# Thresholded attention with approximate screening: another table of the instruction order, and more spare products in the tail

## The chip, the cores and the metric

The kernel runs on one core of a Trainium2 chip. The metric is the device time of one launch in microseconds (us). A core has five engines with instruction streams of their own: TensorE (PE in the profile; PEld is its weight load), VectorE (DVE), ScalarE (ACT), GpSimd (POOL) and SyncE (SP, which here only issues DMAs). Each stream is executed in order; engines wait for each other and for DMAs through semaphores.

## The reference

For 8 x 12 heads, 512 queries and keys, and dimension 64:

```python
scores = np.einsum('bhqd,bhkd->bhqk', Q, K) / sqrt(64)
weights = softmax(scores)                      # over the keys
weights = np.where(weights > 0.1, weights, 0)
weights = weights / (weights.sum(-1) + 1e-10)
out = np.einsum('bhqk,bhkd->bhqd', weights, V)
```

With random normal inputs hardly any weight exceeds 0.1, so almost every row of the output is zero.

## The kernel before, in words

The kernel screens all rows cheaply, and computes exactly only those rows that may hold a weight over the threshold.

**The screen.** Work is cut into 24 *units* of four heads (two head pairs); unit 0 is loaded in two halves. For each unit, SP loads K (`k`, four DMAs at L398) and Q (`q`, L403) and writes zeros to that unit's part of the output (`z`, L626). POOL casts and scales Q to 16 bits (`qcast`, L411, two instructions). PE transposes K (`ktr`, L421) and Q (`qtr`, L432). ACT or DVE copies K from PSUM to a tile `kt` (`kev`), POOL casts it into the tile `qk` (`kh`, L391), and ACT or DVE copies Q there (`qev`; these copies stand at L387 for ACT and L389 for DVE). For each head pair and each quarter t of the keys, PE multiplies keys by queries (`sc`, L467, two matmuls), and ACT (L475) or DVE (L477) takes the exponential of each half (`ex`); which of the two does it is a letter of the table. PE then sums these exponentials and their eighth powers over the keys into one PSUM bank `acc` (`g`, L496). DVE also makes a bound of the row norms (`bits`, L457), which PE adds (`size`, L503).

**The exact part.** Four units (eight head pairs) form a *group*; there are six, called x0 to x5 here. When the 16 `g` and four `size` of a group are done, DVE reads `acc` (`evac`), and PE and DVE turn it into a list of at most 128 candidate rows (`test`, `flags`, `rank`, `key`, `oh`, `idx`, `idxev`). POOL gathers these rows of Q by an indirect DMA (`gather`, L556), spreads them (`split`, L563), PE transposes them (`xtr`, L568) and multiplies them by the group's keys in f32 (`xqk`, L582, 16 matmuls), ACT takes the exponential (`xexp`), and DVE finds the key over the threshold (`xcut`, `xkeep`, `xvi`, `xoi`). POOL then fetches the rows of V (`gv`, L612, indirect DMA, here called the *fetch*) and writes them over the zeros of the output (`scatter`, L619, indirect DMA), which has to wait until the fetch has landed. Both wait in POOL's stream, so that everything behind them on POOL, the casts `kh` and `qcast` of later units, waits with them.

**The order.** A string `ORDER` lists all 1138 steps: a number of the step, a letter of its engine (A, D, G, P, S for ACT, DVE, POOL, PE, SP), and buffer numbers. `Plan.run` walks through it:

```python
        for token in table.split():
            no, eng, at = re.fullmatch(r"(\d+)([A-Za-z])(.*)", token).groups()
            name, engs, deps, fn, takes, gives = self.ops[int(no)]
            ...
            fn(self.ENGINES[eng])
```

Every instruction is wrapped in `keep`, which asks the framework to hold it behind the one recorded before it on its engine. In the built program PE, DVE, ACT and SP stand exactly as the table lists them; on POOL some indirect DMAs stand one or more steps further ahead than in the table, both before and after the change.

**The tail.** After the last unit only the exact part of x4 and x5 is left, a chain of short steps. Into it the kernel puts products of zeros that nobody reads, which only keep PE busy, 3 behind `rank` of x5 and 14 behind its `idx`:

```python
    def spare(dst, n):
        for _ in range(n):
            keep(nc.tensor.matmul(dst[:], lhsT=idle[:, 0:P], rhs=idle[:], start=True, stop=True))
    ...
    add(("spare", 0), "PE", [("rank", last)], lambda e: spare(acc, 3))
    add(("spare", 1), "PE", [("idx", last)], lambda e: spare(acc, 14))
```

Of the kernel before, what the change touches and what calls it, by code (L numbers as in the profile page):

```python
# [23 lines left out]
182P 180D 181A 218P4.6.9 246D1 221P3.5.8 177A 252P0.2 186S 222A 223D 183P 253A4 220D 224P1.3.7 254A 227P0.5.6
251G0 187D1 332S1 226A 232P2.6.5 225A 229D 188P3 234A 247P 255G2 189D 256P1.5 219D 228A 190P 331S0 191D
235P0.6.4 257A 258D 293P3.4 192D1 236A 238P1.5.3 294D3 230P 295A 231P 239A 233D 296G1 240A 241P0.4.2 394S0
259P1.3.1 237D 242A 193P2 243D 292G1 261A 262P5.6.0 194D2 244P 260A 263D 248S 245P 264A 196G1 195D 287D0
# [54 lines left out]
class Plan:  # L82
# [28 lines left out]
def kernel(  # L111
# [232 lines left out]
    acc = psum.tile([P, SO * P], f32, name="acc")  # L344
# [32 lines left out]
    add = plan.add  # L377
# [455 lines left out]
```

## Time and profile before

| | |
|---|---|
| three runs | 199.59, 201.0, 201.52 us; median 201.0 us |
| the profiled execution | 201.37 us, of which the span from first to last instruction is 199.6 us |
| busy share of the span | PE 85%, DVE 80%, ACT 75%, POOL 43% |
| granted TensorE clock, mean | 0.951 |
| bytes moved by DMA | 38.45 MB; the loads and zero writes end at about 144 us |

The span has three parts: about 20 us until the pipeline is full, the screen up to about 176 us with the exact parts of x0 to x3 inside it, and a tail of 24 us in which the engines wait for each other. A row of a timeline gives start, duration, engine, line, operation, tiles and count, and in brackets the idle time of the engine ahead of it and what ended that. A row of a table of windows gives, for one stretch, the busy time of each engine (with the number of instructions), the granted clock (PEclk), the busy share of the DMA engines and GB/s.

### The profile page before, as it was taken

To read this page: it belongs to the slowest core of one execution; us is meant where nothing else is said; L and a number is where in the kernel's file an instruction comes from. 1 tells how busy PE (TensorE), PEld (TensorE's weight loads), DVE (VectorE), ACT (ScalarE), POOL (GpSimd) and SP (SyncE) were. 2 spreads that over 40 slices of the span, in tenths; PEclk is the share of its full clock that TensorE was granted. 3 is DMA by queue.
4 is the path that set the end of the run, shared out by engine and by line. 5 is a ranking of instruction groups with operands and counts; after the bars stand their busy time and mean duration, and the time that the engine had idled before them with its cause. 6 is when DMAs were issued, how large, how long until landed. Compare 5 with 4: busy or idle time off the path is not lost.

```text
span 199.6 us, 5872 instructions
## 1 busy us (share of the span) xinstructions
PE 169.8 (85%) x2266; PEld 69.7 (35%) x2266; DVE 160.3 (80%) x335; ACT 149.6 (75%) x303; POOL 86.6 (43%) x129
## 2 busy tenths in 40 slices
PE   7798999999899999999699999979729899977610
PEld 2343344443433434335234354334103534323100
DVE  7578999999799989999897999968907999972040
ACT  2769999999599999899597999958817898920010
POOL 8644435385085554342941855423440602305222
PEclk9979999999999999999999999999966999999785
DMA  5999999999899998999988768988800000000000
GB/s 139 254 252 255 302 283 255 338 324 287 247 247 347 325 291 181 272 275 236 252 231 256 221 183 242 288 290 227 361 4 0 5 0 3 7 0 11 1 2 10
DMA packets 67440, 38.45 MB, mean 193 GB/s; under 512 B 51882, under 2 KB 64240, under 8 KB 67408
## 3 DMA queue, kind: packets, MB, share of 16 engines
q1 hardware_dynamic: 66560, 37.50, 67.0%
q8 instruction: 19, 0.31, 0.7%
q0 software_dynamic: 576, 0.27, 0.6%
q10 hardware_dynamic: 272, 0.26, 0.5%
q14 instruction: 13, 0.11, 0.2%
HBM read 25.56 MB, written 12.78 MB: 192 GB/s over the span
## 4 chain that ended last, share of the span: by engine, by line
PE 44%; DVE 16%; ACT 13%; issue 11%; DMA 9%; POOL 4%; POOLq 0%; SPq 0%; DVEq 0%; ACTq 0%
PE bank L467 16%; PE acc L496 15%; ACT e L475 9%; DVE e L477 8%; PE bank L421 5%; PE bank L582 4%; DMA qs<-in_Q_dram,idx 4%; DMA vr<-in_V_dram,idx 4%; DVE v L457 3%; ACT kt L387 3%; DMA k<-in_K_dram 2%; POOL qk L391 2%; PE acc L503 2%; POOL out_dram L619 1%; DVE qk L389 1%
## 5 line engine op out<-in xcount | busy, mean ns | idle before, releaser
L475 ACT ACTIVATE e<-bank 128x512 f16<-128x512 f32 x232 | 121.5, 621 | 15.5 <-PE bank L467 15.1
L477 DVE TENSOR_SCALAR e<-bank 128x512 int16<-128x512 f32 x152 | 96.9, 680 | 10.1 <-PE bank L467 9.8
L467 PE MATMUL bank<-qk 64*128 64x512 f16 x384 | 68.0, 389 | 10.6 <-POOL qk L391 5.9
L496 PE MATMUL acc<-e,w_sum 128*32 128x512 f16 x384 | 57.8, 391 | 0.0
L496 PE MATMUL acc<-e,w_pow 128*32 128x512 bf16 x384 | 57.8, 391 | 0.0
L411 POOL TENSOR_SCALAR qh<-q 128x512 f16<-128x512 f32 x48 | 32.8, 683 | 17.1 <-DMA q<-in_Q_dram 13.0
L391 POOL CAST qk<-kt 128x1024 f16<-128x1024 f32 (+1 forms) x24 | 24.9, 1040 | 27.8 <-ACT kt L387 16.3
L467 PEld LDWEIGHTS <-qk 64*128 64x128 f16 x384 | 18.6, 95 | 47.8 <-issue 36.3
L387 ACT COPY kt<-bank 128x512 f32<-128x512 f32 (+1 forms) x35 | 19.9, 590 | 6.7 <-PE bank L421 6.5
L496 PEld LDWEIGHTS <-w_sum 128*32 128x32 f16 x384 | 13.8, 96 | 26.6 <-issue 22.1
L457 DVE TENSOR_SCALAR v<-qk 128x1024 int32<-128x1024 int32 x24 | 20.6, 860 | 2.8 <-POOL qk L391 1.1
L612 POOL DMA_INDIRECT vr<-in_V_dram,idx x6 | 7.2, 1193 | 27.9 <-DVE oks L738 6.4
L421 PE MATMUL bank<-identity_f,k 64*128 64x64 f32 x384 | 17.9, 233 | 0.4 <-DMA k<-in_K_dram 0.4
L421 PEld LDWEIGHTS bank<-identity_f,k 64*128 64x128 f32 x384 | 15.6, 145 | 6.2 <-issue 2.7
L496 PEld LDWEIGHTS <-w_pow 128*32 128x32 bf16 x384 | 13.6, 96 | 1.0 <-issue 0.7
L619 POOL DMA_INDIRECT out_dram<-vr,idx x6 | 6.7, 1120 | 15.7 <-PE bank L432 6.1
L582 PE MATMUL bank<-kt,xq 128*32 128x512 f32 x96 | 13.0, 663 | 0.4 <-ACT xq L387 0.4
L389 DVE COPY qk<-bank 128x512 f16<-128x512 f16 (+1 forms) x33 | 12.8, 409 | 0.4 <-PE bank L432 0.4
L556 POOL DMA_INDIRECT qs<-in_Q_dram,idx x6 | 7.1, 1188 | 10.6 <-DVE idx L546 8.1
L503 PE MATMUL acc<-v,w_size 128*32 128x512 bf16 x96 | 9.5, 385 | 1.8 <-DVE v L457 1.8
L432 PEld LDWEIGHTS <-qh 64*128 64x128 f16 x384 | 8.5, 95 | 6.1 <-issue 3.1
L432 PE MATMUL bank<-identity_h,qh 64*128 64x64 f16 x384 | 10.1, 191 | 0.5 <-POOL qh L411 0.2
(95 smaller groups left out, 105.1 us busy)
## 6 DMA issues: line engine op xcount, KB each, us to landing
k<-in_K_dram SPq DMA_DIRECT2D x96, 128.0 KB, 4.2
out_dram<-zero SPq DMA_DIRECT2D x24, 512.0 KB, 6.0
q<-in_Q_dram SPq DMA_DIRECT2D x23, 512.0 KB, 6.2
q<-in_Q_dram ACTq DMA_DIRECT2D x1, 256.0 KB
q<-in_Q_dram SPq DMA_DIRECT2D x1, 256.0 KB
qs<-in_Q_dram,idx POOLq DMA_INDIRECT x6, 4.8
vr<-in_V_dram,idx POOLq DMA_INDIRECT x6, 4.1
out_dram<-vr,idx POOLq DMA_INDIRECT x6, 3.6
```

What stands on the lines that cost most here:

```text
L387: keep(nc.scalar.copy(dst, src))
L389: keep(nc.vector.tensor_copy(dst, src))
L391: keep(nc.gpsimd.tensor_copy(dst, src))
L411: keep(nc.gpsimd.tensor_scalar(dst, src, ALPHA, 1.0, op0=ALU.mult, op1=ALU.mult))
L421: keep(nc.tensor.matmul(bank_at(("kp", u), i)[:, c:c + D], lhsT=src[ps, n0 + n, r, :], rhs=identity_f32[ps, ps], is_transpose=True, start= ...
L432: keep(nc.tensor.matmul(bank_at(("qp", u), i)[:].bitcast(f16)[:, c:c + D], lhsT=src[ps, n0 + n, r, :], rhs=identity_h[ps, ps], is_transpos ...
L457: keep(nc.vector.tensor_scalar(v_b[at("v", q)][:].rearrange("p a n c -> p (a n c)").bitcast(i32), qk_b[at("qk", q)][:].rearrange("p a n c ...
L467: keep(nc.tensor.matmul(bank_at(("sc", hp, t), h)[:], lhsT=qk[ps, 1, n, t * P:(t + 1) * P], rhs=qk[ps, 0, n, :], start=True, stop=True))
L475: keep(nc.scalar.activation(dst, src, ACTF.Exp, scale=math.log(2.0) / 1024.0, bias=exp_bias))
L477: keep(nc.vector.tensor_scalar(dst.bitcast(i16), src, EXP_BIAS * 1024.0, 0.0, op0=ALU.add, op1=ALU.max))
L496: keep(nc.tensor.matmul(acc[32 * j:32 * j + 32, :], lhsT=w, rhs=rhs, **turn(x, j)))
L582: keep(nc.tensor.matmul(bank_at(("xs", x))[32 * b:32 * b + 32, :], lhsT=xq[:, a * P + 32 * b:a * P + 32 * b + 32], rhs=kt_b[at("kt", GQ * ...
```

## The change

`ORDER` is replaced by another table of the same 1138 steps. The table was searched for under the assumption that gathers and fetches land late by a fixed time. In it the `scatter` steps stand further behind their fetches (63 steps instead of 22 for x3, 61 instead of 39 for x0), six more exponentials are on DVE instead of ACT (158 and 226, before 152 and 232), so are five more `kev` copies (20, before 15), and three more `qev` copies are on ACT (20, before 17). The spare products in the tail are 6 and 17 instead of 3 and 14.

```diff
 ORDER = """
-12S3 13A2 0G 5G 37S 7G 11D 2G 38S 1D 6G 64S2 3G 10D 8G 15P0.1 14G1 16A9 18D3 19A 4G 20P2.3 17A 40P4.5 21A 65S1
...
+12S3 13A2 5G 37S 2G 11D 0G 6G 38S 1D 64S2 7G 8G 10D 3G 15P0.1 14G1 16A9 18D3 19A 9G 20P2.3 17A 40P4.5 21A 65S1
...
-    add(("spare", 0), "PE", [("rank", last)], lambda e: spare(acc, 3))
-    add(("spare", 1), "PE", [("idx", last)], lambda e: spare(acc, 14))
+    add(("spare", 0), "PE", [("rank", last)], lambda e: spare(acc, 6))
+    add(("spare", 1), "PE", [("idx", last)], lambda e: spare(acc, 17))
```

What this does to the streams of POOL and SP is seen in the built program at three places. The tiles of unit n count down: `kt9` is unit 0's, `kt1` unit 8's, `kt0` unit 9's, and then from `kt9` again.

POOL around the exact part of x0, before (from `split` of x0 to the `kh` of unit 9):

```order
L563 TENSOR_TENSOR qb1_184<-qs1_182,ix2_177 128x128
L391 CAST qk0_150<-kt2_142 128x1024
L612 DMA vr2_191<-in_V_dram,idx2_180 128x64
L391 CAST qk3_153<-kt1_141 128x1024
L411 TENSOR_SCALAR qh0_138<-q2_137 128x512 x2
L619 DMA out_0_dram<-vr2_191,idx2_180 8192x64
L411 TENSOR_SCALAR qh1_139<-q1_136 128x512 x2
L391 CAST qk2_152<-kt0_140 128x1024
```

The same place in the changed program, from the `kh` of unit 7 to the `gather` of x1:

```order
L391 CAST qk0_150<-kt2_142 128x1024
L563 TENSOR_TENSOR qb1_184<-qs1_182,ix2_177 128x128
L411 TENSOR_SCALAR qh1_139<-q0_135 128x512 x2
L411 TENSOR_SCALAR qh0_138<-q2_137 128x512 x2
L411 TENSOR_SCALAR qh1_139<-q1_136 128x512 x2
L612 DMA vr2_191<-in_V_dram,idx2_180 128x64
L619 DMA out_0_dram<-vr2_191,idx2_180 8192x64
L391 CAST qk3_153<-kt1_141 128x1024
L391 CAST qk2_152<-kt0_140 128x1024
L556 DMA qs0_181<-in_Q_dram,idx1_179 128x64
```

The `kh` of unit 7 has moved ahead of `split`, the three `qcast` of units 8, 9 and 10 stand ahead of the fetch, and the `scatter` stands directly behind its fetch, ahead of the `kh` of units 8 and 9. (In the table both `kh` stand ahead of the `scatter`; in the built program they do not.)

POOL around the exact part of x3, before (from `split` of x3, with the `kh` of units 19, 20 and 21):

```order
L563 TENSOR_TENSOR qb0_183<-qs0_181,ix2_177 128x128
L411 TENSOR_SCALAR qh0_138<-q2_137 128x512 x2
L391 CAST qk0_150<-kt8_148 128x1024
L612 DMA vr2_191<-in_V_dram,idx2_180 128x64
L411 TENSOR_SCALAR qh1_139<-q1_136 128x512 x2
L619 DMA out_0_dram<-vr2_191,idx2_180 32768x64
L391 CAST qk3_153<-kt1_141 128x1024
L391 CAST qk2_152<-kt0_140 128x1024
```

The same place in the changed program:

```order
L563 TENSOR_TENSOR qb0_183<-qs0_181,ix2_177 128x128
L411 TENSOR_SCALAR qh0_138<-q2_137 128x512 x2
L391 CAST qk0_150<-kt8_148 128x1024
L411 TENSOR_SCALAR qh1_139<-q1_136 128x512 x2
L391 CAST qk3_153<-kt1_141 128x1024
L612 DMA vr2_191<-in_V_dram,idx2_180 128x64
L619 DMA out_0_dram<-vr2_191,idx2_180 32768x64
L391 CAST qk2_152<-kt0_140 128x1024
```

Here too the `scatter` now stands directly behind its fetch, but the `kh` of unit 20 (`kt1`) stands ahead of both; what is queued behind them is the `kh` of unit 21 (`kt0`).

SP in the first 30 us, before (loads of Q and K, and zeros to the output; `q2` is the buffer of unit 3, `k0` that of unit 3, `k3` that of unit 4):

```order
L398 DMA k0_131<-in_K_dram 128x4x64 x4
L403 DMA q2_137<-in_Q_dram 128x4x256
L626 DMA out_0_dram<-zero_73 128x1024
L398 DMA k3_134<-in_K_dram 128x4x64 x4
L403 DMA q1_136<-in_Q_dram 128x4x256
```

The same place in the changed program:

```order
L398 DMA k0_131<-in_K_dram 128x4x64 x4
L398 DMA k3_134<-in_K_dram 128x4x64 x4
L403 DMA q2_137<-in_Q_dram 128x4x256
L626 DMA out_0_dram<-zero_73 128x1024 x2
L403 DMA q1_136<-in_Q_dram 128x4x256
```

The K load of unit 4 has moved ahead of the Q load of unit 3.

More of the change, by code (lines that the diff above doesn't have):

```diff
@@ L24 @@
[L24 to L27, printed above, removed]
-265P0.4.13 297P1.3 266A 268P2.5.12 267D 288P 333G0 298A 289S 271P 269D 270A 273P0.6.11 299D 276P1.4.10 275A 274D
@@ L79 @@
+1067P 1088D 1086A 1090P1.6.8 1095P0.5.7 1089D 1091A 1093P 1096A 1097D 1098P2.4.6 1101P1.3.5 1092A 1100D
+1104P0.5.4 937G1 1099A 1094P 1105D 1106A 938P6 1102D 1103A 1107P 939D1 1108P 1135D 940P4 1112D0 1113P2 941A1
+1114D 1115P 942D 943D 1133P 944D 945D 1116D 946G1 1117D0 1136D 1118P0 1119D0 1134P 1120D 1121G0 1122G0 1123P5
+1124A0 1125P1 1126A0 947G 1127D 1128D 1129D 1137D 1131G0 1130D 1132G
 """
```

119 lines of the change are left out of this document (60 added, 59 removed).

## The prediction

> **What bounds the kernel now.** I read the page's totals first, then a table of windows, to see where the engines fall behind their own pace.
>
> ```profile
> span 199.6 us, 5872 instructions
> PE 169.8 (85%) x2266; PEld 69.7 (35%) x2266; DVE 160.3 (80%) x335; ACT 149.6 (75%) x303; POOL 86.6 (43%) x129
> ...
> 0.00:20.00 20.00, 16.33 (x183) 6.79 (x183) 14.05 (x51) 13.29 (x28) 12.00 (x42) 0.91 0.87 225
> 20.00:50.00 30.00, 28.96 (x423) 12.08 (x422) 29.76 (x53) 28.93 (x59) 15.56 (x19) 1.00 1.06 298
> 20.00:130.00 110.00, 104.43 (x1507) 43.75 (x1505) 103.44 (x193) 100.47 (x203) 55.61 (x65) 1.00 0.97 268
> 144.00:153.00 9.00, 4.74 (x38) 1.20 (x40) 3.04 (x5) 2.88 (x7) 2.14 (x2) 0.62 0.03 7
> 153.00:175.70 22.70, 21.58 (x315) 9.75 (x313) 21.82 (x41) 20.25 (x41) 5.86 (x7) 1.00 0.01 3
> 175.70:199.60 23.90, 10.66 (x72) 3.57 (x64) 6.20 (x25) 1.64 (x5) 5.99 (x6) 0.81 0.02 5
> ```
>
> In the screen three engines are nearly full at once: from 20 to 130 us PE is busy 95%, DVE 94%, ACT 91% (104.43, 103.44 and 100.47 of 110 us). There is one hole, 144 to 153 us, in which DVE works 3.04 of 9 us. The tail, 23.9 us, is a chain. So there are three questions: what becomes of the hole, whether the new table opens another, and what the tail gains.
>
> The hole is seen in the timelines of POOL and PE, where the exact part of x3 stands:
>
> ```profile
> 139.47 1.10 POOL L612 DMA_INDIRECT vr<-in_V_dram,idx  x1 [3.01 <-DVE idx L608]
> 140.64 1.31 POOL L411 TENSOR_SCALAR qh<-q 128x512 f16<-128x512 f32 x2
> 146.05 1.10 POOL L619 DMA_INDIRECT out_dram<-vr,idx  x1 [4.09 <-issue]
> 147.17 1.04 POOL L391 CAST qk<-kt 128x1024 f16<-128x1024 f32 x1
> 148.26 1.03 PE L467 MATMUL bank<-qk 64*128 64x512 f16 x4 [4.75 <-POOL qk L391]
> ```
>
> The fetch of x3 is issued at 139.47; the scatter behind it waits for its landing and starts at 146.05; the `kh` of unit 20 stands behind the scatter, and PE idles 4.75 us for that `kh`. The DMA view gives the landings of the fetches of x0, x1, x2 and x3, in us from issue:
>
> ```profile
> vr<-in_V_dram,idx POOLq DMA_INDIRECT x1, 4.2
> ...
> vr<-in_V_dram,idx POOLq DMA_INDIRECT x1, 7.7
> ...
> vr<-in_V_dram,idx POOLq DMA_INDIRECT x1, 3.4
> ...
> vr<-in_V_dram,idx POOLq DMA_INDIRECT x1, 5.7
> ```
>
> For x3, 139.47 + 5.7 = 145.17, and the scatter starts 0.88 later. From its start to the end of the `kh` it is 147.17 + 1.04 - 146.05 = 2.16. So a `kh` directly behind a scatter is done at *fetch + landing + 3.0 us*. This is the price that I use below.
>
> **The change, part by part.** The sum is made against the profiled execution, 201.37 us (span 199.6 and 1.77 around it), which lies 0.4 us above the median of the three runs, 201.0.
>
> *x3: -5.8 us.* Unit 20's `kh` now stands ahead of the fetch. Behind fetch and scatter is unit 21's, which PE needs 25 exponentials after `xvi` of x3 in the table (counted there from `xvi` to unit 21's first `sc`). 384 exponentials in 175.7 us are 0.46 us each, so PE gets there some 11 us after the fetch; the `kh` is done after 5.7 + 3.0 = 8.7, or 10.7 with the longest landing seen. The hole goes. What it is worth: 4.75 us of idle PE, and behind it the clock is low (0.62 in that window). DVE did 3.04 us of work in these 9 us, for which it needs 3.04 / (21.82/22.70) = 3.2 us at the pace of the window behind; 9.0 - 3.2 = 5.8.
>
> *x1: -1.1 us.* The same, smaller:
>
> ```profile
> 84.81 1.10 POOL L612 DMA_INDIRECT vr<-in_V_dram,idx  x1 [3.10 <-DVE idx L608]
> ...
> 93.44 1.24 POOL L619 DMA_INDIRECT out_dram<-vr,idx  x1 [6.13 <-PE bank L432]
> ...
> 95.79 0.39 PE L467 MATMUL bank<-qk 64*128 64x512 f16 x2 [1.11 <-POOL qk L391]
> ```
>
> The landing of 7.7 us holds up the `kh` of unit 13 until PE has lost 1.11 us. In the new table the fetch of x1 comes 40 exponentials ahead of unit 13's first `sc` instead of 21, so this wait goes. The fetches and scatters of x2 and x4 keep enough behind them (x2: 25 exponentials from `xvi` to the first `sc` of unit 17) and are put at nothing.
>
> *x0: +3.3 us, a new wait.* Now the scatter of x0 stands directly behind its fetch, and behind it the `kh` of units 8 and 9 and the gather of x1. Unit 8's first `sc` on PE waits for that `kh`, and ACT and DVE then wait for PE.
>
> ```profile
> 50.43 1.90 PE L582 MATMUL bank<-kt,xq 128*32 128x512 f32 x16
> ...
> 54.72 1.30 POOL L612 DMA_INDIRECT vr<-in_V_dram,idx  x1 [5.10 <-DVE idx L603]
> ...
> 60.12 0.38 PE L467 MATMUL bank<-qk 64*128 64x512 f16 x2
> ```
>
> From the start of `xqk` of x0 (50.43) to the fetch it is 4.29 us, and to unit 8's first `sc` (60.12) 9.69 us, with 20 exponentials between in the old table. The new one has 18 between, so PE gets there after 9.69 x 18/20 = 8.7 us. The `kh` is done after 4.29 + 4.2 + 3.0 = 11.5. PE idles 2.8 us; with the landings of x2 and x1, 3.4 and 7.7, it is 2.0 or 6.3. The three `qcast` ahead of the fetch fit in the 4.3 us (1.31 for one, above) if their Q has landed. For x3 a hole of 4.75 cost 5.8 in all; of this surplus of 1.05 I take half, since here the clock may hold: 2.8 + 0.5. On the other hand unit 7's `kh` no longer waits behind `split` of x0; that is worth something between nothing and the wait of `split`:
>
> ```profile
> 48.14 0.40 POOL L563 TENSOR_TENSOR qb<-qs,ix 128x128 f32<-128x128 f32 x1 [1.89 <-DMA qs<-in_Q_dram,idx]
> ```
>
> PE is busy with other things then, so -0.2 of the possible -1.9.
>
> *Loads at the start: +0.5 us.* Unit 4's K goes ahead of unit 3's Q on SP.
>
> ```profile
> 16.37 1.68 SPq L403 DMA_DIRECT2D q<-in_Q_dram  x1
> ...
> 18.69 3.37 SPq L398 DMA_DIRECT2D k<-in_K_dram  x4
> ...
> 21.81 1.64 POOL L411 TENSOR_SCALAR qh<-q 128x512 f16<-128x512 f32 x2 [2.35 <-DMA q<-in_Q_dram]
> ...
> 27.04 0.61 PE L467 MATMUL bank<-qk 64*128 64x512 f16 x4 [0.30 <-DVE qk L389]
> ```
>
> The four issues of K take 3.37 us, so the Q lands and its `qcast` starts near 25.2 instead of 21.81. The cast ended 3.6 us before unit 3's first `sc` at 27.04; that slack is used up almost to the last, and the new table puts this `sc` two exponentials later (0.9 us). The cost lies between 0 and 3.4; I take 0.5, near the end where the slack covers it. The zero writes that move later have nothing waiting soon. The constants that POOL makes in another order at the start change the same few us either way: 0.
>
> *More work on DVE: +1.0 us.* The groups by shape give the time of one:
>
> ```profile
> L477 DVE TENSOR_SCALAR e<-bank 128x512 int16<-128x512 f32 x152 | 96.9, 680 | 10.1 <-PE bank L467 9.8
> ...
> L389 DVE COPY qk<-bank 128x512 f16<-128x512 f16 x32 | 12.6, 413 | 0.4 <-PE bank L432 0.4
> L389 DVE COPY kt<-bank 128x512 f32<-128x512 f32 x14 | 9.4, 683 | 0.6 <-ACT e L475 0.3 <-PE bank L421 0.2
> ```
>
> Six exponentials (96.9/152 = 0.64), five copies of K (9.4/14 = 0.67) and three copies of Q less (12.6/32 = 0.39) make 3.8 + 3.4 - 1.2 = 6.0 us. ACT loses about as much. The cost lies between 0, if it fills DVE's idle time (110 - 103.44 = 6.6 us from 20 to 130), and 6.0, where DVE is full as from 20 to 50 us (29.76 of 30). I take 1.0, nearer the longer window.
>
> *Tail: -1.45 us.* In the built program scatter of x4 still stands ahead of split of x5, so the chain keeps its steps:
>
> ```profile
> 175.30 1.95 PE L582 MATMUL bank<-kt,xq 128*32 128x512 f32 x16
> ...
> 178.26 0.81 PE L200 MATMUL acc<-idle 128*128 128x512 f16 x3
> ...
> 180.78 3.18 PE L200 MATMUL acc<-idle 128*128 128x512 f16 x14
> ...
> 185.49 0.40 POOL L563 TENSOR_TENSOR qb<-qs,ix 128x128 f32<-128x128 f32 x1
> 185.95 0.33 PE L568 MATMUL bank<-identity_f,qb 128*128 128x128 f32 x1 [1.99 <-POOL qb L563]
> ...
> 186.63 3.40 PE L582 MATMUL bank<-kt,xq 128*32 128x512 f32 x16 [0.35 <-ACT xq L387]
> ...
> 187.00:188.00 1.00, 1.00 (x8) 0.22 (x4) 0.00 (x0) 0.00 (x0) 0.00 (x0) 0.50 0.00 0
> ```
>
> The 14 products take 3.18 us, 0.23 each; three more end at 184.6, ahead of `xtr` at 185.95, so they delay nothing; the three more behind `rank` start at 179.1 and end near 179.8, before the one-hot tile of x5 is ready (`idx` at 180.26). What they may bring: `xqk` of x5 took 3.40 us at half clock, that of x4 1.95 at full clock, and the low clock came after an idle gap of 1.99 us. With a gap of 1.3 us I take it that the clock holds: 1.95 - 3.40 = -1.45.
>
> By the Trainium skill, "TensorE: Matmul & The Clock Gate", section "HAM oscillation — how this bites in real kernels", only idle gaps above about 3.4 us matter. By that rule the gap of 1.99 us would have done no harm and the added products would bring nothing; the row at 187 us speaks against it, with the clock at 0.50 although no gap ahead of it was as long.
>
> **Sum:** -5.8 - 1.1 + 3.3 - 0.2 + 0.5 + 1.0 - 1.45 = -3.75; 201.37 - 3.75 = **197.6 us**.
>
> **The rivals.** *A, the new wait is long.* If the fetch of x0 lands as late as that of x1 did (7.7), PE idles 6.3 us instead of 2.8: 201.1. For it: POOL reaches that fetch while SP loads K of several units. Against it: the fetch of x0 had K loads around it before too, and took 4.2.
>
> *B, the tail's clock falls anyway:* 197.6 + 1.45 = 199.1. The gap shrinks by only 0.7 us, and no row tells how short it must be for the clock to hold.
>
> *C, slower: DVE becomes the bound.* Up to 175.7 DVE works 160.3 - 6.2 = 154.1 us, 140.0 of them after the first 20; with 6.0 more it is 146.0. If its share stays at the 94.0% of the window from 20 to 130, these take 155.3 us; with the first 20, the x0 wait of 3.3, 0.5 at the start, the tail of 23.9 - 1.45 and 1.77 around, the time is 203.3. Below a share of 94.2% the kernel is over 203.0, more than 1% slower than the median. For it: that share is a measured one and DVE has no other engine's slack to live on. Against it: the 94% contain waits that go, and from 20 to 50 us DVE reached 99%. The forecast asks for 97.7%.
>
> *D, nothing bites at x0 and DVE's work is hidden:* a landing of 3.4, no surplus, the other terms at nothing: 197.6 - 1.3 - 0.5 - 1.0 = 194.8.
>
> *E, the change does not do what it says:* the scatters were put further behind in the table, but stand directly behind their fetches on POOL. At x3 it would need a landing over 8 us to bring the wait back; none was seen.
>
> **How the numbers follow.** Forecast (195.5 to 199.5) 0.5; A 0.15; B 0.1; C 0.1; D 0.12; E 0.03, near A's time. About 1% is what a measurement of this kernel tells from no change, 199.0 to 203.0 around 201.0. Faster: most of the forecast (0.43), D and some of B: 0.6. Same: the rest of the forecast, A, E and most of B: 0.3. Slower: 0.1, C. The range is 193.5 (D with a little more) to 202.0 (A and a little more), which leaves out C and half of the far sides.
>
> **What would show it.** After: POOL's timeline has the scatter of x0 starting about 0.9 us after its fetch has landed, and PE's first `sc` of unit 8 with an idle time of 2 to 6 us "<-POOL qk"; no such row near 95 and 148 us; the granted clock 1.00 at 140 to 155 us; `xqk` of x5 about 1.95 us; DVE's share of the screen up to 96 to 98%. The prediction is wrong if PE waits at a place that I have put at nothing (Q of units 3, 9 or 10, or a gather), or if DVE stays near 94% with no wait to name.

## The result, and the profile after

The changed kernel takes **193.1 us** (median of four runs, 192.7 to 194.2) against 200.5 us for the kernel before; the ratio is 0.964, with a 95% interval from 0.957 to 0.970. The forecast was 197.6, with a range from 193.5: the direction was right, the gain was about twice what was predicted, and the time lies just under the range. The kernel before itself took between 195 and 205 us in all the runs of this study, so a ratio with its interval compares only the quicker runs of both kernels and can differ from the ratio of two medians.

The totals of the page after, and its table of windows for the stretches that were shown of before:

```profile
span 192.4 us, 5896 instructions
PE 170.1 (88%) x2272; PEld 69.7 (36%) x2272; DVE 164.3 (85%) x343; ACT 146.7 (76%) x295; POOL 86.2 (45%) x129
...
20.00:50.00 30.00, 27.53 (x388) 11.16 (x390) 27.17 (x49) 24.58 (x49) 13.68 (x16) 0.94 0.93 271
20.00:130.00 110.00, 102.59 (x1461) 42.06 (x1463) 101.29 (x189) 94.22 (x190) 55.08 (x65) 0.97 0.92 263
144.00:153.00 9.00, 8.48 (x125) 3.78 (x124) 9.00 (x17) 8.87 (x18) 3.96 (x6) 1.00 0.32 122
153.00:170.80 17.80, 16.98 (x226) 6.70 (x223) 17.80 (x33) 15.92 (x31) 4.75 (x5) 1.00 0.01 4
170.80:192.40 21.60, 11.24 (x86) 4.43 (x85) 7.55 (x28) 1.64 (x5) 5.53 (x6) 0.83 0.02 5
```

The hole at 144 to 153 us is gone: DVE is full there (9.00 of 9 us) and up to 170.8 us, and the clock is 1.00. From 20 to 50 us it got worse: PE 27.53 instead of 28.96, ACT 24.58 instead of 28.93.

A finer ruler is the end of the n-th exponential, counted in order of time over both engines; both kernels have 384. The pieces between are worked out from the two profiled executions:

| exponentials | before, us | after, us | difference | what stands there |
|---|---|---|---|---|
| 1 to 32 | 22.09 | 20.82 | -1.3 | start; 20.5 to 22.6 in all profiles of both tables |
| 33 to 64 | 11.81 | 15.17 | +3.4 | unit 4's K ahead of unit 3's Q |
| 65 to 128 | 27.36 | 27.81 | +0.5 | |
| 129 to 160 | 12.65 | 16.45 | +3.8 | new wait behind the scatter of x0 |
| 161 to 192 | 14.23 | 13.50 | -0.7 | |
| 193 to 240 | 23.15 | 19.24 | -3.9 | x1: wait for the `kh` of unit 13; copies of K |
| 241 to 288 | 18.36 | 20.11 | +1.8 | |
| 289 to 320 | 14.68 | 13.67 | -1.0 | x3: wait of `xtr` for `split` |
| 321 to 336 | 12.35 | 5.50 | -6.9 | x3: wait for the `kh` of unit 20 |
| 337 to 384 | 18.42 | 18.48 | +0.1 | |
| 384 to the end | 24.47 | 21.62 | -2.9 | tail |

The differences add up to -7.2, the difference of the two spans. Most of these pieces repeat within about 1 us from one profiled execution of a table to the next, so an edit can be judged in its own piece even where the whole time varies by more. Not so the 193rd to 240th of the old table (23.15 to 25.89 where no edit touched them), and of the new one the 33rd to 64th (12.74 to 15.17 with K first), the 129th to 160th (16.01 to 17.82 with the wait at x0) and the 241st to 288th (18.82 to 22.58).

The places where the waits were: POOL at x3, then POOL and PE at x0, with the landing of the fetch of x0 from the DMA view:

```profile
143.00 1.04 POOL L391 CAST qk<-kt 128x1024 f16<-128x1024 f32 x1 [1.73 <-DVE kt L389]
144.19 1.10 POOL L612 DMA_INDIRECT vr<-in_V_dram,idx  x1 [0.15 <-issue]
150.01 1.02 POOL L619 DMA_INDIRECT out_dram<-vr,idx  x1 [4.72 <-DVE e L477]
151.04 1.05 POOL L391 CAST qk<-kt 128x1024 f16<-128x1024 f32 x1
...
59.01 1.11 POOL L612 DMA_INDIRECT vr<-in_V_dram,idx  x1 [1.69 <-DMA k<-in_K_dram]
63.28 1.02 POOL L619 DMA_INDIRECT out_dram<-vr,idx  x1 [3.16 <-DMA vr<-in_V_dram,idx]
64.30 1.05 POOL L391 CAST qk<-kt 128x1024 f16<-128x1024 f32 x1
...
65.40 0.70 PE L467 MATMUL bank<-qk 64*128 64x512 f16 x4 [1.88 <-POOL qk L391]
...
vr<-in_V_dram,idx POOLq DMA_INDIRECT x1, 4.0
```

At x3 the `kh` of unit 20 is done before the fetch is issued, and the `kh` behind the scatter, at 151.04, holds up nobody. At x0 the wait that was forecast is there: 4.0 us after the fetch, its scatter; behind it the `kh` of unit 8; PE idles 1.88 us. The granted clock is 0.50 from 65.8 to 69.2.

At the start, SP, POOL and PE after:

```profile
12.67 7.90 SPq L398 DMA_DIRECT2D k<-in_K_dram  x7
20.66 0.57 SPq L403 DMA_DIRECT2D q<-in_Q_dram  x1
...
26.65 1.32 POOL L411 TENSOR_SCALAR qh<-q 128x512 f16<-128x512 f32 x2 [3.44 <-DMA q<-in_Q_dram]
...
27.33 0.29 PE L432 MATMUL bank<-identity_h,qh 64*128 64x64 f16 x8 [1.10 <-POOL qh L411]
```

The Q of unit 3 is issued at 20.66 (before: in a group from 16.37), its `qcast` starts at 26.65 instead of 21.81, and PE waits for it.

The tail, from the indices of x4 to `xqk` of x5, first of the kernel before (the rows not shown yet), then of the changed one:

```profile
179.01 0.21 DVE L608 TENSOR_SCALAR idx<-accs,ix 128x1 int32<-128x1 f32 x1
179.14 0.20 DVE L603 TENSOR_SCALAR idx<-accs,ix 128x1 int32<-128x1 f32 x1
179.51 0.69 DVE L532 TENSOR_TENSOR oh<-slot_no,keys 128x1024 f16<-128x1024 bf16 x1
179.62 1.50 POOL L612 DMA_INDIRECT vr<-in_V_dram,idx  x1 [6.16 <-DVE keys L528]
184.45 1.01 POOL L619 DMA_INDIRECT out_dram<-vr,idx  x1 [2.00 <-DMA qs<-in_Q_dram,idx]
```

```profile
174.89 0.21 DVE L603 TENSOR_SCALAR idx<-accs,ix 128x1 int32<-128x1 f32 x1
175.02 0.20 DVE L608 TENSOR_SCALAR idx<-accs,ix 128x1 int32<-128x1 f32 x1
175.38 1.04 POOL L612 DMA_INDIRECT vr<-in_V_dram,idx  x1 [9.67 <-DVE keys L528]
175.39 0.71 DVE L532 TENSOR_TENSOR oh<-slot_no,keys 128x1024 f16<-128x1024 bf16 x1
178.64 1.02 POOL L619 DMA_INDIRECT out_dram<-vr,idx  x1 [0.30 <-issue]
179.82 0.40 POOL L563 TENSOR_TENSOR qb<-qs,ix 128x128 f32<-128x128 f32 x1 [0.17 <-DMA qs<-in_Q_dram,idx]
180.96 1.92 PE L582 MATMUL bank<-kt,xq 128*32 128x512 f32 x16 [0.35 <-ACT xq L387]
```

Besides the clock (`xqk` 1.92 instead of 3.40) something moved that the forecast had left out. L603 writes the index of the fetch and L608 that of the scatter; in the new table the index of the fetch comes first, and in every profile the fetch of x4 starts 0.48 or 0.49 us behind the start of L603. The scatter of x4 comes 3.3 us after its fetch, before 4.8, and no longer stands in the way of `split` of x5: from the fetch of x4 to that `split` it is 4.44 us, before 185.49 - 179.62 = 5.87. The DMA view has the fetch of x4 landing in 2.3 us, before in 4.0. The records of the DMA packets show one on the instruction queue, 16 KB, from 181.36 for 1.12 us in the kernel before, 0.4 us ahead of the fetch's first packets (181.75); of the 16 parts of the fetch the last is done at 183.66, 1.14 us after the other fifteen. After the change the same packet comes at 177.23, 0.2 us behind the fetch's first packets (177.05), and all is done at 177.68.

### The profile page after: what moved, and what is told of

The parts are those of the page before. It is cut to its first block, busy times and chain, and to the rows that moved or that the text cites. A ratio compares the mean times of both kernels' runs of the same rounds, so it can differ in the third digit from the quotient of the medians.

```text
span 192.4 us, 5896 instructions
## 1 busy us (share of the span) xinstructions
PE 170.1 (88%) x2272; PEld 69.7 (36%) x2272; DVE 164.3 (85%) x343; ACT 146.7 (76%) x295; POOL 86.2 (45%) x129
## 4 chain that ended last, share of the span: by engine, by line
PE 40%; DVE 29%; DMA 11%; issue 9%; POOL 6%; SPq 2%; ACT 1%; POOLq 0%; DVEq 0%; ACTq 0%
DVE e L477 16%; PE bank L467 15%; PE acc L496 13%; DVE v L457 5%; DMA k<-in_K_dram 5%; PE bank L582 4%; PE bank L421 3%; DMA q<-in_Q_dram 3%; POOL qh L411 3%; DVE kt L389 2%; DMA vr<-in_V_dram,idx 2%; PE acc L503 2%; DVE qk L389 2%; PE bank L432 2%; POOL qk L391 2%
## 5 line engine op out<-in xcount | busy, mean ns | idle before, releaser
L475 ACT ACTIVATE e<-bank 128x512 f16<-128x512 f32 x226 | 118.5, 613 | 11.9 <-PE bank L467 11.0
L477 DVE TENSOR_SCALAR e<-bank 128x512 int16<-128x512 f32 x158 | 101.3, 682 | 4.7 <-PE bank L467 4.2
L411 POOL TENSOR_SCALAR qh<-q 128x512 f16<-128x512 f32 x48 | 34.1, 710 | 21.9 <-DMA q<-in_Q_dram 7.8
L387 ACT COPY kt<-bank 128x512 f32<-128x512 f32 (+1 forms) x30 | 17.1, 588 | 7.6 <-PE bank L421 6.9
L457 DVE TENSOR_SCALAR v<-qk 128x1024 int32<-128x1024 int32 x24 | 19.0, 795 | 2.7 <-POOL qk L391 1.9
L612 POOL DMA_INDIRECT vr<-in_V_dram,idx x6 | 6.5, 1084 | 22.1 <-DVE keys L528 9.7
L389 DVE COPY kt<-bank 128x512 f32<-128x512 f32 (+1 forms) x20 | 13.0, 659 | 1.5 <-PE bank L421 0.8
L389 DVE COPY qk<-bank 128x512 f16<-128x512 f16 (+1 forms) x30 | 11.7, 411 | 1.8 <-PE bank L432 1.4
L387 ACT COPY qk<-bank 128x512 f16<-128x512 f16 (+1 forms) x20 | 10.9, 566 | 2.2 <-PE bank L432 2.2
L432 PE MATMUL bank<-identity_h,qh 64*128 64x64 f16 x384 | 10.5, 192 | 2.0 <-POOL qh L411 1.8
L432 PEld LDWEIGHTS <-qh 64*128 64x128 f16 x384 | 8.8, 96 | 9.1 <-POOL qh L411 4.6
L582 PE MATMUL bank<-kt,xq 128*32 128x512 f32 x96 | 11.6, 597 | 0.4 <-ACT xq L387 0.4
```

Source lines behind the costliest of these rows:

```text
L387: keep(nc.scalar.copy(dst, src))
L389: keep(nc.vector.tensor_copy(dst, src))
L411: keep(nc.gpsimd.tensor_scalar(dst, src, ALPHA, 1.0, op0=ALU.mult, op1=ALU.mult))
L432: keep(nc.tensor.matmul(bank_at(("qp", u), i)[:].bitcast(f16)[:, c:c + D], lhsT=src[ps, n0 + n, r, :], rhs=identity_h[ps, ps], is_transpos ...
L457: keep(nc.vector.tensor_scalar(v_b[at("v", q)][:].rearrange("p a n c -> p (a n c)").bitcast(i32), qk_b[at("qk", q)][:].rearrange("p a n c ...
L475: keep(nc.scalar.activation(dst, src, ACTF.Exp, scale=math.log(2.0) / 1024.0, bias=exp_bias))
```

## The experiments

The times are medians with the lowest and the highest run; "before" is the median of the kernel before in the same series on the same chip. e1 to e4 ran on one chip, e5 to e12 on a second, e13 to e16 on a third; the changed kernel itself was run again on the third alone (e15).

| run | us | before | ratio, 95% |
|---|---|---|---|
| e1_before_spares | 199.3 (196.4 to 203.2) | 198.8 | 1.008 (0.999 to 1.017) |
| e2_before_kh20 | 194.8 (194.4 to 195.0) | 198.8 | 0.986 (0.977 to 0.995) |
| e3_after_q3 | 191.2 (190.4 to 191.7) | 198.8 | 0.969 (0.960 to 0.978) |
| e4_after_pin_x0 | 192.2 (190.5 to 192.6) | 198.8 | 0.971 (0.959 to 0.982) |
| e5_after_both | 189.5 (188.9 to 191.7) | 199.0 | 0.954 (0.944 to 0.964) |
| e6_before_xoi | 199.9 (195.3 to 201.5) | 199.0 | 0.991 (0.979 to 1.004) |
| e7_after_spares3 | 194.0 (193.3 to 194.4) | 199.0 | 0.973 (0.966 to 0.980) |
| e8_before_kh13 | 198.3 (196.6 to 200.6) | 199.0 | 1.001 (0.996 to 1.007) |
| e9_before_three | 190.7 (190.2 to 191.6) | 200.7 | 0.957 (0.943 to 0.970) |
| e10_after_letters | 196.4 (194.0 to 198.1) | 200.7 | none |
| e11_before_k4 | 207.0 (202.5 to 209.2) | 200.7 | none |
| e12_after_xvi | 195.1 (192.9 to 198.2) | 200.7 | 0.973 (0.948 to 0.997) |
| e13_after_ex | 195.0 (193.1 to 196.2) | 201.7 | 0.963 (0.949 to 0.976) |
| e14_after_copies | 194.4 (193.9 to 198.0) | 201.7 | 0.967 (0.957 to 0.976) |
| e15_after_again | 193.5 (191.9 to 196.1) | 201.7 | 0.960 (0.949 to 0.972) |
| e16_both_again | 193.2 (190.3 to 194.7) | 201.7 | 0.952 (0.937 to 0.968) |

### x3 and x1, in the table of before

e2 does the change at x3 alone, here in the stream of POOL:

```diff
+L411 TENSOR_SCALAR qh_139<-q_136 128x512 x2
+L391 CAST qk_153<-kt_141 128x1024
 L612 DMA vr_191<-in_V_dram,idx_180 128x64
-L411 TENSOR_SCALAR qh_139<-q_136 128x512 x2
 L619 DMA out_dram<-vr_191,idx_180 32768x64
-L391 CAST qk_153<-kt_141 128x1024
```

> The table of before, with the kh of unit 20 ahead of the fetch of x3 and the scatter of x3 directly behind its fetch, as in the changed program; nothing else. Theory: PE's wait of 4.75 us at 148 us and the half clock behind it go, evac x3 to evac x4 takes 28.5 us or less instead of 34.2, the time falls by 5.8 us. Rival D (DVE or PE is the bound there and the work only moves): by less than 3 us. Rival M (unit 21's kh, now directly behind the scatter, makes PE wait instead): a wait of 1 to 3 us at the first sc of unit 21 and a gain of 3 us or less.

POOL of e2, with the `kh` of unit 20, the fetch and the `kh` of unit 21, which waits for ACT and not for the scatter:

```profile
141.75 1.04 POOL L391 CAST qk<-kt 128x1024 f16<-128x1024 f32 x1 [0.66 <-DVE kt L389]
142.94 1.10 POOL L612 DMA_INDIRECT vr<-in_V_dram,idx  x1 [0.15 <-issue]
...
148.97 1.04 POOL L391 CAST qk<-kt 128x1024 f16<-128x1024 f32 x1 [1.06 <-ACT kt L387]
```

The 321st to 336th exponential take 5.84 us instead of 12.35, and PE has no idle gap over 0.8 us there any more. So x3 is worth 6.5 us in its own place, the largest part of the change's gain. The whole time falls by less, from 198.8 to 194.8, with a ratio of 0.986; why this edit and most other single ones move the whole time by less than their own pieces was not found.

e8 moves the scatter of x1 behind the `kh` of units 13 and 14:

```diff
-L619 DMA out_dram<-vr_190,idx_179 16384x64
 L391 CAST qk_152<-kt_146 128x1024
 L391 CAST qk_151<-kt_145 128x1024
+L619 DMA out_dram<-vr_190,idx_179 16384x64
```

> The kernel before with the scatter of x1 behind the kh of units 13 and 14 instead of ahead of both. As predicted for x1: the wait of 1.11 us near 95.8 goes, -1.1 us. Rival (this wait is what the 193rd to 240th exponential lose in all against the changed kernel, 23.2 against 19.2 us): -2.5 to -4 us. Second rival (other engines fill the wait): no change.

The 193rd to 240th take 21.16 us instead of 23.15: -2.0, between the forecast and its first rival. In e9, which has the same edit beside others, the piece takes 21.29. That of the kernel before is the shortest without the edit: in e1, e2, e6 and e11 it takes 23.66 to 25.89, each time with a clock of 0.50 for 3.4 or 6.8 us in it, so there the difference is 2.4 to 4.7. In e2 and e11 the longest wait of PE in it is another (2.42 and 2.46 us for the one-hot tile), so not all of that need be x1. In the whole time e8 can't be told from the spread of this kernel (median -0.7, ratio 1.001).

### The start and x0

e3 and e11 exchange the two loads on SP, in the changed kernel and in the kernel before; the diff is that of e3 (in e11 K also passes the zero write that stood between the two):

```diff
+L403 DMA q_137<-in_Q_dram 128x4x256
 L398 DMA k_134<-in_K_dram 128x4x64 x4
-L403 DMA q_137<-in_Q_dram 128x4x256
```

> The changed kernel with the Q load of unit 3 ahead of the K load of unit 4 on SP, as before. Theory L (the late Q cost 2 us or more, with the half clock that it brought at 28 us): sc of unit 3 starts at 27 us instead of 29.2, the clock stays at 1.00 from 12 us on, evac of x0 is 1.5 to 2.5 us earlier, and the time 1.5 to 2.5 us below the changed kernel (190.5 to 191.5). Rival (the wait of x0 or DVE takes it up later): evac of x0 earlier, the time within 0.7 us of the changed kernel.

> The kernel before with the K load of unit 4 ahead of the Q load of unit 3 on SP, as in the changed kernel. As predicted: +0.5 us, qcast of unit 3 starts near 25.2. Theory from the changed kernel, where the exchange back gave 1.9 us and the 33rd to 64th exponential took 12.7 us instead of 15.2: these take 13.5 to 15 instead of 11.8, +2 to +3 us, the larger value if the clock falls behind the wait.

With Q first, the 33rd to 64th exponential of the changed kernel take 12.69 instead of 15.17 us, and its time is 191.2. But 15.17 is the longest of eight profiles of the new table with K first; the others take 12.74 to 14.75 (median of the eight 14.0), and the three with Q first (e3, e5, e16) 12.34 to 12.69. With K first, those of the kernel before take 15.10 instead of 11.81 (11.73 to 11.92 in the other profiles of the old table). Its median rises by 6.3, to 207.0, its lowest run by 4.8, to 202.5; the part beyond the 3.3 of this piece lies elsewhere and was not taken apart (in the profiled execution the 193rd to 240th take 25.89). In e11 the `qcast` starts at 24.75, where the forecast had it, and PE waits 1.92 us for it:

```profile
24.75 1.31 POOL L411 TENSOR_SCALAR qh<-q 128x512 f16<-128x512 f32 x2 [6.06 <-DMA q<-in_Q_dram]
25.43 0.29 PE L432 MATMUL bank<-identity_h,qh 64*128 64x64 f16 x8 [1.92 <-POOL qh L411]
```

The waiting instruction is `qtr` (L432), which runs well ahead of the first `sc` on which the forecast had measured the slack; and the clock is 0.50 from 26.7 to 30.2.

e4 holds the scatter of x0 behind the `kh` of units 8 and 9:

```diff
 L612 DMA vr_191<-in_V_dram,idx_180 128x64
-L619 DMA out_dram<-vr_191,idx_180 8192x64
 L391 CAST qk_153<-kt_141 128x1024
 L391 CAST qk_152<-kt_140 128x1024
+L619 DMA out_dram<-vr_191,idx_180 8192x64
```

> The changed kernel with the scatter of x0 held where the table has it, behind the kh of units 8 and 9; nothing else. Theory W (that scatter stalls PE by 1.9 us and halves the clock for 3.4 us behind it): no wait at 65 us, clock 1.00 there, evac x0 to evac x1 takes 27 us instead of 30.0, the time 2.5 to 3.5 us below the changed kernel (189.5 to 190.5). Rival (the loads of K and Q or DVE are the limit there): evac x1 earlier by 1 us or less, the time within 1 us of the changed kernel.

Now the `kh` of unit 8 follows the fetch, and the scatter comes 7.6 us later:

```profile
61.23 1.03 POOL L391 CAST qk<-kt 128x1024 f16<-128x1024 f32 x1 [0.17 <-DVE kt L389]
...
68.85 1.29 POOL L619 DMA_INDIRECT out_dram<-vr,idx  x1 [0.15 <-issue]
```

The 129th to 160th take 13.06 instead of 16.45: -3.4. The new wait is real and costs in its place what it was forecast to cost. The whole time, 192.2, does not show it: against the kernel before on the same chip the ratio is 0.971 (e3: 0.969), no lower than the 0.964 of the changed kernel, so neither repair alone is shown to make the whole kernel quicker.

e5 has both repairs, e16 again on another chip, beside e15, the changed kernel itself.

> The changed kernel with two edits together: on SP the Q load of unit 3 ahead of the K load of unit 4 again, and on POOL the scatter of x0 held behind the kh of units 8 and 9. Theory (the two losses of the changed kernel are separate waits): the gains add, about -1.9 and -1.5 us on 193.1, so 189.5 to 190.0; no PE gap near 64 us, and the 128th exponential ends near 61 us, the 160th near 75. Rival (both losses are one, or what one gives the other takes): 191 to 192, as with either edit alone.

> The changed kernel with the Q load of unit 3 ahead of the K load of unit 4 and the scatter of x0 behind the kh of units 8 and 9, on the same chip as the changed kernel. Theory (two separate waits, 1.9 and 1.5 us): 3 to 4 us below it, 189.5. Rival (the earlier 189.46 was owed to its chip): 1 to 2 us below it.

> The changed kernel once more, as the base of the others on this chip: 193.1 us by its first runs, 192 to 195 by the chip and by whether the clock falls behind the wait at x0.

On the chip of e5 the time is 189.5, the lowest of all versions. On that of e16 both pieces are as short again (12.35 and 13.11), but other waits come up in the profiled execution (194.0 us), above all 1.93 us at `size` with a fall of the clock behind it (the 241st to 288th take 22.58 instead of 20.47), and the median, 193.2, is hardly below the 193.5 of the changed kernel. Over both versions' eight runs, each on two chips, the medians are 191.0 and 193.2; the ratios to before are 0.954 and 0.952, with intervals up to 0.964 and 0.968, against 0.964 and 0.960. So the repaired version is some 2 us below the changed kernel by the medians, but not on every chip.

### The tail

e6 and e12 exchange the two index instructions of x4 on DVE, in the kernel before as it is after, and the other way round. (The expectations of e6, e9 and e12 name the two the wrong way about: L603 is the index of the fetch.)

```diff
+L603 TENSOR_SCALAR idx_179<-accs,ix_176 128x1
 L608 TENSOR_SCALAR idx_179<-accs,ix_176 128x1
-L603 TENSOR_SCALAR idx_179<-accs,ix_176 128x1
```

> The kernel before with two DVE instructions of x4 exchanged in the tail: the index of the scatter (L603) ahead of that of the fetch (L608), as in the changed kernel. Theory (the fetch of x4 lands late because a 16 KB packet of instructions, which a DMA engine loads for 1.1 us, comes 0.4 us ahead of its packets on one engine): the fetch is issued 0.1 us earlier and ahead of DVE's one-hot instruction, lands in 2.3 to 2.6 us instead of 4.0, the scatter of x4 starts about 1.1 us earlier, and split of x5 is 8.4 to 8.8 us behind evac of x5 instead of 9.75; -1 us. Rival (the landing of 4.0 belongs to the order of other things in this table): it stays at 4.0, split at 9.7, no change.

> The changed kernel with the two DVE instructions of x4 in the tail exchanged: the index of the fetch (L608) ahead of that of the scatter (L603), as in the kernel before. Theory (the fetch is then issued behind the start of the one-hot instruction and meets the 16 KB packet of instructions): landing 3.8 to 4.2 instead of 2.3, scatter of x4 behind the landing of the gather, split of x5 9.2 to 9.7 behind evac of x5 instead of 7.6 to 7.8, +1.3 to +1.8 us: 194.4 to 195. Rival (the landing belongs to the rest of the table): 2.3, 193.1.

e6 first, then e12, POOL and the one-hot instruction of DVE:

```profile
180.76 1.04 POOL L612 DMA_INDIRECT vr<-in_V_dram,idx  x1 [5.92 <-DVE keys L528]
180.78 0.71 DVE L532 TENSOR_TENSOR oh<-slot_no,keys 128x1024 f16<-128x1024 bf16 x1
184.02 1.01 POOL L619 DMA_INDIRECT out_dram<-vr,idx  x1 [0.30 <-issue]
185.41 0.39 POOL L563 TENSOR_TENSOR qb<-qs,ix 128x128 f32<-128x128 f32 x1 [0.38 <-DMA qs<-in_Q_dram,idx]
```

```profile
174.38 0.69 DVE L532 TENSOR_TENSOR oh<-slot_no,keys 128x1024 f16<-128x1024 bf16 x1
174.48 1.50 POOL L612 DMA_INDIRECT vr<-in_V_dram,idx  x1 [9.65 <-DVE keys L528]
179.21 1.01 POOL L619 DMA_INDIRECT out_dram<-vr,idx  x1 [1.91 <-DMA qs<-in_Q_dram,idx]
180.25 0.41 POOL L563 TENSOR_TENSOR qb<-qs,ix 128x128 f32<-128x128 f32 x1
```

Two instructions of 0.2 us, exchanged, switch the whole pattern on and off. The fetch starts 0.01 us ahead of the one-hot instruction or 0.11 us behind its start; the issue of the fetch takes 1.04 or 1.50 us, it lands in 2.4 or 3.9 us, and `split` of x5 stands 8.40 us behind `evac` of x5 instead of 9.75 (e6), or 9.07 instead of 7.6 to 7.8 as in the changed kernel and e3 to e5 (e12). In e12 the tail from the 384th exponential takes 23.16 us, in the nine other profiles of the changed table with 6 and 17 products 21.62 to 21.97: +1.2 to +1.5. In the whole time e12's median is 1.5 to 2 us above those of the changed kernel, on another chip, and e6 is not to be told from before. In the old table only a part of the gain reaches the end: in the profile of e6 the 14 products ran at half clock and held up `xtr` of x5 by some 0.9 us, and e9, which has the same edit, shows the same (4.72 us, 0.8 us). The tail from the 384th exponential takes 22.59 us in e6 and 22.47 in e9, in e1, e2, e8 and e11 22.95 to 23.27. The row of e6:

```profile
182.05 4.87 PE L200 MATMUL acc<-idle 128*128 128x512 f16 x14
```

e1 and e7 change the spare products alone:

```diff
-    add(("spare", 0), "PE", [("rank", last)], lambda e: spare(acc, 3))
-    add(("spare", 1), "PE", [("idx", last)], lambda e: spare(acc, 14))
+    add(("spare", 0), "PE", [("rank", last)], lambda e: spare(acc, 6))
+    add(("spare", 1), "PE", [("idx", last)], lambda e: spare(acc, 17))
```

> The table of before with the change's spare products (6 and 17). Theory S (the spare products keep the clock up in the tail and do nothing else): xqk of x5 takes 1.95 us instead of 3.40, the tail from evac of x5 to the end is 22.4 us instead of 23.9, the time 1 to 1.5 us below before. Rival T (the tail was shorter after the change because the fetch of x4 landed sooner, 2.3 instead of 4.0 us, which the spares have no part in): the tail keeps split of x5 at 9.7 us behind evac of x5, and of the 3.7 us at most 1.5 come back. Rival N (the clock does not depend on three more products): no change.

> The changed kernel with 3 and 14 spare products instead of 6 and 17. Theory (in the new tail the gap on PE ahead of xtr of x5 is short anyway, since split comes 2.1 us earlier): the 14 products end about 0.3 us ahead of xtr, the clock stays at 1.00, xqk of x5 takes 1.9 us, the time is the same within 0.5 us. Rival (the added products hold the clock): a gap near 0.9 us, xqk of x5 3.4 us, +1.5 us.

Added to the kernel before they move nothing that can be measured (199.3 against 198.8); without them the changed kernel loses nothing in the tail either: from the 384th exponential it takes 21.94 us, and `xqk` of x5 keeps the full clock (its time is 194.0, on a chip on which the changed kernel itself was not run):

```profile
179.65 0.33 PE L568 MATMUL bank<-identity_f,qb 128*128 128x128 f32 x1 [0.62 <-POOL qb L563]
180.33 1.92 PE L582 MATMUL bank<-kt,xq 128*32 128x512 f32 x16 [0.36 <-ACT xq L387]
```

Of the six profiles of the old table with 3 and 14 products (before, e2, e6, e8, e9, e11), only that of the kernel before has 3.40 us there; the others have 1.92, e8 with an idle gap of 1.87 ahead of it.

### The work moved to DVE

e10 gives ACT back six exponentials and five copies of K, and DVE three copies of Q; e13 the exponentials alone, e14 the copies alone. One step of each kind (the letter is the engine, D or A):

```diff
-979D 664D5 258A
+979A 664A5 258D
```

> The changed kernel with its work for DVE and ACT divided in the old numbers: six exponentials (three between the 64th and the 160th, three behind the 320th) and five copies of K (between the 192nd and the 288th) back on ACT, three copies of Q back on DVE, all at their places. As predicted (the added work on DVE costs 1.0 us): 192.1. Rival 1 (the added DVE work is hidden or balances the engines): 193 to 195, no gain; rival 2 (DVE is the bound where it is full, 144 to 170 us, and the three exponentials there are worth 0.64 each): -1.9 in that stretch.

> The changed kernel with six exponentials back on ACT (three between the 64th and the 160th, three behind the 320th), the copies as changed. Forecast's theory (work on DVE costs time; six of 0.64 us are the larger half of it): 0.6 us below the changed kernel on the same chip. Rival (ACT with its copies and exponentials is as near to the limit as DVE, and the exponentials are what the changed kernel gains by): +1 to +3 us, with 19 us or more for the 337th to 384th exponential instead of 18.5.

> The changed kernel with five copies of K back on ACT (units 14 to 18) and three copies of Q back on DVE (units 5, 7, 9), the exponentials as changed. Forecast's theory: 0.4 us below the changed kernel on the same chip. Rival (the copies of K on DVE let ACT keep its pace): +0.5 to +2 us, lost between the 192nd and the 288th exponential, which took 39.4 us.

| | 193 to 240 | 321 to 336 | 337 to 384 | all, us |
|---|---|---|---|---|
| e15, as changed | 19.01 | 5.50 | 18.77 | 193.5 |
| e13, exponentials back | 19.43 | 4.97 | 19.38 | 195.0 |
| e14, copies back | 20.27 | 5.50 | 18.75 | 194.4 |
| e10, all back | 20.31 | 4.97 | 19.38 | 196.4 |

The copies of K cost about 1 us when they are back on ACT (20.27 and 20.31 from 193 to 240, in the other profiles of the new table 19.01 to 19.72). The exponentials behind the 320th give and take the same (24.35 against 24.27). The medians all lie above that of the changed kernel, with overlapping spreads, and e10 ran on another chip than the rest. No part of the moved work costs time on DVE; what it brings is about 1 us, and beyond that nothing is settled.

### The three waits together

e9 is the kernel before with e2, e8 and e6 together.

> The kernel before with the three edits of POOL and of the tail together: kh of unit 20 ahead of the fetch of x3, scatter of x1 behind the kh of units 13 and 14, index of the scatter ahead of that of the fetch in x4. All else is the table of before: its start, its division of work between ACT and DVE, its 3 and 14 spare products. Theory (these three waits make nearly all that the changed kernel gains): 194.8 with the first edit alone, -2.0 at x1, -1.35 in the tail: 191 to 192.5, no slower than the changed kernel. Rival (the new table as a whole is better paced): 193.5 to 195, a wait moves elsewhere.

190.7 us, 10 below the median of before on the same chip (ratio 0.957), and 2 to 3 below the changed kernel on other chips (0.964 and 0.960). Against the profile of before its pieces differ by -6.5 (x3), -1.9 (x1) and -2.0 (tail), and by -1.6 in the first 32 exponentials, which no edit touched; of the tail's -2.0 some 1.5 is the half clock under `xqk` that only that one profile of before had. In the whole time the edits one by one gave 4.0 (e2), 0.7 (e8) and nothing (e6) by the medians, which is less than 10: the parts add up in their pieces, not in the whole times. Three moves of single steps are thus enough for all that the new table gains, and more; what the new table does at the start and at x0 takes a part of it back.

## Why the prediction was wrong in size

The mechanisms at x3, x1 and x0 were right, with x1 too small. Four steps failed: the slack at the start, the cost of the work on DVE, the tail that keeps its steps, and a wait at x3 that was put at nothing. Rival D's time, 194.8, came nearest, but by chance: its condition that nothing bites at x0 did not hold. The sizes below are those of the pieces; in the whole time the single edits show less.

**x3, -5.8.** Right; 6.5 by e2, 6.9 between the two profiles.

**x1, -1.1.** Right in kind, too small: 2.0 by e8, and up to 4.7 against executions in which the clock fell in that stretch, where other waits take part. The forecast took only the 1.11 us of PE's wait; of e8's gain 1.2 us lie in the 16 exponentials that held the wait (7.50, before 8.68) and 0.8 in the next 16 (5.14, before 5.94).

**x0, +3.3 - 0.2.** Right: +3.8 between the profiles, -3.4 by e4. The `kh` of unit 8 was done 11.65 us behind the start of `xqk`, with 11.5 forecast, but PE got there after 9.8 instead of 8.7, so it idled 1.88 us instead of 2.8. The piece grew by more than the idle time, as forecast, but by 1.9 us more instead of 0.5. The clock, which fell behind it, is a small part of that: where it held (e3, e10, e13, e14) the piece still took 16.01 to 16.38 us, against 13.02 to 13.11 with the scatter held back. That the sum came out near is in part luck.

**Loads at the start, +0.5.** Too small: +2.5 by e3 in the two executions compared, +1.7 by the median of the eight profiles with K first, +3.3 by e11. The step that failed is "that slack is used up almost to the last": the slack was measured at the first `sc`, but what waits for the cast is `qtr`, ahead of it (1.92 us in e11, 1.10 after the change). In the new table this `qtr` stands behind 46 exponentials instead of 41, so it can wait less there than in e11.

**Work on DVE, +1.0.** The step that failed is that the cost lies between 0 and 6.0: it was a gain of about 1 by e14, from the copies of K that ACT no longer makes, and nothing from the exponentials. That is of the size of the spread, but no sign of a cost was seen. DVE's share from 20 to 130 us did not rise to 96 to 98% either, it is 92% (101.29 of 110), beside the waits named here. Rival C did not come about: from 153.0 to 170.8 us DVE is busy all the time.

**Tail, -1.45.** The step that failed is "the chain keeps its steps". The order of steps on POOL was kept, but their times were not, since the two index instructions on DVE had changed places: the fetch of x4 lands in 2.3 us instead of 4.0, and that is worth 1.2 to 1.5 us in the new table (e12) and 1.35 at `split` in the old one (e6). The 1.45 of the forecast, the clock under `xqk` of x5, was a chance of one profiled execution (one of six; e8 had a gap of 1.87 us ahead of `xqk` and kept the full clock), and the added products bring nothing measurable (e1, e7). So the term had nearly the size of a real one and none of its cause; between the two profiles both count, -2.9.

**Put at nothing:** the wait of `xtr` of x3 for its `split`, by which the gather of x3, landing in 7.2 us, held up PE:

```profile
134.02 0.33 PE L568 MATMUL bank<-identity_f,qb 128*128 128x128 f32 x1 [1.16 <-POOL qb L563]
...
133.16 0.40 POOL L563 TENSOR_TENSOR qb<-qs,ix 128x128 f32<-128x128 f32 x1 [3.25 <-PE acc L496]
```

The first row is of the kernel before, the second of the changed one, where the gather landed in 4.2 and 22 exponentials stand between it and `split` instead of 20. The 289th to 320th take 14.1 to 14.9 us in all profiles of the old table and 13.67 in those of the new: -1.0. The quicker landing is not needed for it: in e7 and e14 the gather landed in 6.2 and 6.4 us, and the piece took 13.67 all the same, so the longer distance in the table is enough there. No experiment took this wait apart.

The errors, in us against the forecast: x3 -0.7, x1 -0.9, DVE -2, `xtr` of x3 -1.0, tail none by size (-1.4 in the profiled execution), start +1.2 to +2.8, x0 nothing. That makes -1.8 to -3.4, beside the 3.65 by which the change of the median (-7.4) went beyond the sum (-3.75). What is left, up to 2 us, is of the size of this kernel's spread; the +1.8 at the 241st to 288th, which works against it (18.8 to 22.6 in other profiles of the new table), was not looked into.

## What to carry to other kernels

Before a term is taken from a stall or a clock in one profiled execution, ask whether it belongs to the program or to that execution: here one of two low clocks was in every profile with that wait (x3) and the other in one of six (the tail). In a chain in which engines wait for each other, a step's order is not its time: follow every transfer on it, and what else the DMA engines carry at that moment. The slack of a late load is measured at the first instruction that reads its cast, not at the one that ends the chain.

## What the runs showed of the hardware

An indirect DMA on POOL took 1.50 us to issue where DVE's one-hot instruction (0.69 us, f16 from bf16, 128x1024) had begun 0.10 to 0.11 us before it (before, e1, e2, e8, e11, e12), and 1.04 where it began 0.01 to 0.02 behind (the twelve other profiles). The Trainium skill, "SBUF — State Buffer", section "SBUF: two separate sides", says that POOL writes such descriptors itself and that DVE in some modes locks it out of a shared pair of ports; by that rule the later one waits until the first is done, here 0.58 us at most; the 0.46 us more that were measured agree.

In the same six profiles a packet of 16 KB on the instruction queue, which took 0.9 to 1.1 us, came 0.02 to 0.4 us ahead of the fetch's packets, and one of the fetch's 16 parts landed 1.0 to 1.35 us behind the other fifteen. In the twelve others the packet came 0.15 to 0.21 us behind the first of them, and the last part landed less than 0.2 us behind the one before it. That the packet held up the DMA engine of the late part fits these times; the records do not name the engine.

The length of an idle gap on PE did not decide whether the clock falls. At the wait of x0, gaps of 1.88, 2.03, 2.04 and 2.94 us (after, e12, e15, e7) were followed by 3.4 us, in e7 6.8 us, at a clock of 0.50; gaps of 1.90, 2.36, 2.58 and 2.83 us (e13, e14, e10, e3) were not. Where it fell for 3.4 us, that piece took 16.39 to 16.79 us, in e7 17.82, and where it did not, 16.01 to 16.38, so the fall itself cost at most 0.8 us, the double one at most 1.8. By the section "HAM oscillation — how this bites in real kernels" of the page "TensorE: Matmul & The Clock Gate" of the Trainium skill, cited in the prediction, none of these gaps should have had an effect; four of eight had one.

What counts is seen on a fixed grid. Where a profile has more than one low stretch (fourteen have), these begin whole multiples of 3.41 us apart (before: 9.44, 145.97, 186.93 and 193.76), and all but the last of each profile last 3.41 us or a multiple of it. All 18 profiles were cut on their own grid, which their first low stretch gives, from 15 us to the end of `xqk` of x5. Of 844 pieces of 3.41 us at full clock, 11 had PE busy for less than 45%, and the clock fell behind every one; 807 had it busy for more than 67%, and it fell behind none; of the 26 between it fell behind 11. At x0 the piece ahead of the fall had PE busy for 1.06 to 1.54 us (e7, e12, e15, after); the emptiest piece at that wait in the others for 1.77 to 2.13 (e3, e10, e14, e13). So these profiles have a gap count by how empty it leaves a whole piece of the grid, and not by its own length; what decides between 45% and 67% stays open.
